# Loading 768 rows at a time instead of 384 in a diagonal prefix-sum kernel that streams 285 MB

## Chip, cores, metric

One core of a Trainium2 chip. Kernels are compared only within the same rounds. The metric is the device time of that core in microseconds. The span of a profile, from its first to its last instruction, is mostly some 1.7 us shorter than the time of the same run.

## The reference

```python
def setup_inputs():
    B, H, W = 4, 4224, 4224
    return {"x": np.random.randn(B, H, W).astype(np.float32)}

def reference(x):
    ps = np.cumsum(np.cumsum(x, axis=1), axis=2)
    diag = np.diagonal(ps, axis1=1, axis2=2)
    return np.cumsum(diag, axis=1).astype(np.float32)
```

Every value below or above the diagonal counts, so all of x, 4 x 4224 x 4224 x 4 = 285.47 MB, has to be read; the result is 68 KB.

## The kernel before

Rows are loaded in groups of 384 (3 to a partition), converted to bf16 on the way, into six rotating buffers. TensorE (PE) sums columns into a small matrix `d` of one row per group; VectorE (DVE) and ScalarE (ACT) share the row sums left of the diagonal; GpSimd (POOL) issues the loads. At the end of a batch the row sums are turned into `d`, and two scans give the output. The last 128 rows of the last batch come in pieces so that little is left to do after the final byte.

```python
P = 128; F = 3; GW = P * F; NG = N // GW; NBUF = 6          # GW = 384, NG = 11
def load_group(b, g):
    t = strips.tile([P, F, N], BF16, name="strip")
    r0 = g * GW
    nc.gpsimd.dma_start(
        out=t, in_=x[b, r0 : r0 + GW, :].rearrange("(p f) w -> p f w", f=F))
    return t
# ... per group g of a batch
for j in range(g + 1, NG):
    for q in range(F):
        columns(j, 0, GW, strip[:, q, j * GW : (j + 1) * GW])    # PE, into d
for q in range(F):
    mu = mup.tile([P, GW], BF16, name="mu")
    masked(mu, strip[:, q, lo:hi], um3[q], ru[:, k, q : q + 1])  # DVE
    columns(g, 0, GW, mu)
    if ws > 0:
        act_sum(sa_at(q), strip[:, q, wp:ws])                    # ACT
row_sums(rs_at, strip[:, :, ws:hi])                              # DVE
if not whole and g == 0:
    diag_b = last.tile([P, P], BF16, name="diag_b")
    nc.gpsimd.dma_start(out=diag_b, in_=x[b, TB:N, TB:N])
# ... at the end of a batch
for q in range(F):
    matmul(d[:, q : GW : F], rows[:, :, q], ident)
# ... last 256 + 128 rows of the last batch
acuts = [(1536, N - HC), (0, 1536)]                              # two pieces of 256 rows
bcuts = [(2432, TB), (1024, 2432), (320, 1024), (0, 320)]        # four pieces of 128 rows
# ... row sums, products with arows, then
row_sums(ttot, tsum[:, : n + 2])
matmul(fin_b, ttot, weights[:, 0:P])                             # then add, store
```

## Time and profile before

| | kernel before |
|---|---|
| time, median of the first 3 runs | 669.16 us (669.05 to 669.71) |
| span of the profile | 667.8 us |
| read from HBM over the span | 428 GB/s |
| transfers on the software queue | 50 (7,456 packets) |
| issue to landing of a 384-row load | 82.6 us |

The busy row of the page shows that no compute engine is near its limit (microseconds, share of the span, instructions):

```profile
PE 229.2 (34%) x862; PEld 96.5 (14%) x862; DVE 253.5 (38%) x371; ACT 153.3 (23%) x249; POOL 33.0 (5%) x72
```

### The profile page before, as it was taken

The page shows a single profiled execution, that of the slowest core. Times are in us where ns is not written, and L with a number is a line of the kernel's source. Part 1 is how long each engine was busy: PE and PEld are TensorE (multiplying, and loading weights), DVE is VectorE, ACT ScalarE, POOL GpSimd, SP SyncE. Part 2 cuts the span into 40 slices and gives each one's busy share as a digit, 9 for nine tenths or more (in the row PEclk, how much of TensorE's full clock was granted, in tenths as well). Part 3 has the DMA queues.
Part 4 walks back from the last instruction along what each step waited for, and adds up shares of the span by engine and source line. Part 5 has one row for each costly group of instructions (what it writes and reads, how often), then busy time and mean ns, then how long its engine had stood idle before and what let it go on. Part 6 is the DMA issues. An engine that isn't in the chain of part 4 may idle for free.

```text
span 667.8 us, 2641 instructions
## 1 busy us (share of the span) xinstructions
PE 229.2 (34%) x862; PEld 96.5 (14%) x862; DVE 253.5 (38%) x371; ACT 153.3 (23%) x249; POOL 33.0 (5%) x72
## 2 busy tenths in 40 slices
PE   0444542211155453221125553322112553322225
PEld 0122211000022221100002221110001221111002
DVE  2123334344623333334472222333457222233357
ACT  0001222233301112223330111222342011122235
POOL 5000000000000000000000000000000000000000
PEclk9977665665577766665557777665555777665668
DMA  9999999999999999999999999999999999999997
GB/s 202 217 219 218 219 219 217 217 216 212 211 221 219 219 219 215 217 219 217 219 217 217 210 216 219 219 219 219 214 216 219 219 217 215 216 216 219 217 207 142
DMA packets 7830, 143.23 MB, mean 214 GB/s; under 512 B 989, under 2 KB 1290, under 8 KB 2314
## 3 DMA queue, kind: packets, MB, share of 16 engines
q0 software_dynamic: 7456, 142.47, 99.7%
q1 hardware_dynamic: 362, 0.61, 0.3%
q8 instruction: 6, 0.10, 0.1%
q14 instruction: 6, 0.05, 0.0%
HBM read 285.47 MB, written 0.07 MB: 428 GB/s over the span
## 4 chain that ended last, share of the span: by engine, by line
another core or an unknown queue 54%; DVE 36%; DMA 7%; PE 1%; issue 1%; POOL 0%; DVEq 0%; POOLq 0%
DVE rs L192 24%; DVE mu L195 9%; DMA strip<-in_x_dram 7%; DVE c L329 1%; PE d L175 1%; DVE parts L192 1%; DVE tsum L192 0%; DVE c L195 0%; POOL strip L70 0%; DVE pu L192 0%; PE carry_ps L175 0%; DVE rows L242 0%; DVE rows L243 0%; DVEq L195 0%
## 5 line engine op out<-in xcount | busy, mean ns | idle before, releaser
L175 PE MATMUL d<-strip,sel 128*11 128x384 bf16 x660 | 183.7, 458 | 367.3 <-DMA strip<-in_x_dram 367.3
L187 ACT ACTIVATE dump<-strip 128x192 bf16<-128x192 bf16 (+13 forms) x124 | 140.5, 1133 | 509.6 <-DMA strip<-in_x_dram 506.9
L195 DVE SCALAR_TENSOR_TENSOR mu<-strip,um 128x384 bf16<-128x384 bf16 x129 | 65.2, 556 | 397.8 <-DMA strip<-in_x_dram 397.8
L175 PEld LDWEIGHTS <-sel 128*11 128x11 bf16 x792 | 90.5, 114 | 530.0 <-issue 508.9
L192 DVE TENSOR_REDUCE rs<-strip 128x3 f32<-128x1152 bf16 (+10 forms) x42 | 163.8, 3899 | 0.0
L175 PE MATMUL d<-mu,sel 128*11 128x384 bf16 x129 | 38.6, 409 | 40.6 <-DVE mu L195 40.6
L70 POOL DMA_DIRECT2D strip<-in_x_dram x43 | 22.9, 536 | 536.0 <-PE d L175 297.1
L187 ACT ACTIVATION_READ_ACCUMULATOR dump<-strip 128x1 f32 x124 | 23.1, 186 | 0.0
L175 PE MATMUL d<-ident,rows 128*11 128x128 f32 x24 | 5.2, 378 | 20.3 <-DVE rows L243 19.9
L195 DVE DVE_READ_ACCUMULATOR mu<-strip,um 128x1 f32 x129 | 10.7, 83 | 0.0
L175 PEld LDWEIGHTS d<-ident,rows 128*11 128x11 f32 x24 | 2.5, 117 | 24.5 <-DVE rows L243 15.0
L175 PE MATMUL fold<-strip,ident_h 128*128 128x480 bf16 (+1 forms) x14 | 4.5, 461 | 1.7 <-DMA strip<-in_x_dram 1.7
L192 DVE TENSOR_REDUCE pu<-d 11x1 f32<-11x384 f32 x4 | 2.2, 545 | 5.1 <-PE d L175 5.1
L329 DVE TENSOR_TENSOR_SCAN c<-ones_row,carry,c 11x384 f32<-11x384 f32 x4 | 4.0, 1006 | 0.1
L329 DVE TENSOR_TENSOR_SCAN c<-ones_row,carry,d 11x384 f32<-11x384 f32 x4 | 4.0, 1001 | 0.1
L308 POOL DMA_DIRECT2D strip<-in_x_dram x4 | 2.1, 536 | 36.0 <-DMA strip<-in_x_dram 22.3
L192 DVE TENSOR_REDUCE parts<-strip 128x3 f32<-128x3072 bf16 x1 | 3.4, 3351 | 0.0
L175 PEld LDWEIGHTS <-ident_h 128*128 128x128 bf16 x20 | 2.1, 114 | 5.2 <-issue 4.8
L192 DVE TENSOR_REDUCE tsum<-strip 128x1 f32<-128x384 bf16 (+2 forms) x4 | 2.0, 490 | 1.2 <-DMA strip<-in_x_dram 1.2
L304 POOL DMA_DIRECT2D strip<-in_x_dram x2 | 1.4, 712 | 15.0 <-PE d L175 15.0
L195 DVE SCALAR_TENSOR_TENSOR c<-d,to_end 11x384 f32<-11x384 f32 x4 | 2.1, 535 | 0.0
L175 PE MATMUL carry_ps<-pu,earlier 11*11 11x2 f32 x8 | 0.7, 159 | 4.1 <-DVE c L195 4.1
(61 smaller groups left out, 27.0 us busy)
## 6 DMA issues: line engine op xcount, KB each, us to landing
strip<-in_x_dram POOLq DMA_DIRECT2D x43, 3168.0 KB, 82.6
strip<-in_x_dram POOLq DMA_DIRECT2D x1, 1080.0 KB, 73.8
strip<-in_x_dram POOLq DMA_DIRECT2D x1, 768.0 KB, 76.8
head<-in_x_dram SPq DMA_DIRECT2D x1, 528.0 KB
strip<-in_x_dram POOLq DMA_DIRECT2D x1, 416.0 KB, 64.4
strip<-in_x_dram POOLq DMA_DIRECT2D x1, 352.0 KB, 65.6
strip<-in_x_dram POOLq DMA_DIRECT2D x1, 176.0 KB, 58.0
strip<-in_x_dram POOLq DMA_DIRECT2D x1, 80.0 KB, 43.5
```

Of the source, the lines that this page charges most:

```text
L70: nc.gpsimd.dma_start(out=t, in_=x[b, r0 : r0 + GW, :].rearrange("(p f) w -> p f w", f=F))
L175: nc.tensor.matmul(o, lhsT=lhsT, rhs=rhs, start=start, stop=False, skip_group_check=True)
L187: nc.scalar.activation(out=dump[:, :w], in_=src, func=ACT.Copy, accum_out=acc)
L192: nc.vector.reduce_sum(out=acc, in_=src, axis=AX.X)
L195: nc.vector.scalar_tensor_tensor(out=o, in0=i, scalar=1.0, in1=m, op0=ALU.mult, op1=ALU.mult, accum_out=acc,)
L304: nc.gpsimd.dma_start(out=part_a[:, :2, c0:c1], in_=src_a[:, :, c0:c1])
L308: nc.gpsimd.dma_start(out=part_b[:, 0, c0:c1], in_=x[b, TB:N, c0:c1])
L329: nc.vector.tensor_tensor_scan(out=c12[:, i, :], data0=ones_row, data1=src, initial=carry[:, i : i + 1], op0=ALU.mult, op1=ALU.add,)
```

## The change

Its intent: fewer and larger transfers. 768 rows come in one load, 6 to a partition, in three buffers of the same total size; the sixth, half-size load of a batch stays at 384 rows. Whole batches keep their groups in natural order, which makes their output one store instead of two. The last 128 rows come in three pieces instead of four. Row sums of 768-row strips lie at another place, so they reach `d` through six more matmuls with a 64-column matrix `halves`.

```diff
-    NBUF = 6
+    NBUF = 3
+    NS = NG // 2
-    mup = ctx.enter_context(tc.tile_pool(name="mup", bufs=4))
+    mup = ctx.enter_context(tc.tile_pool(name="mup", bufs=3))
+    def strip_tile():
+        return strips.tile([P, F2, N], BF16, name="strip")
+    def load_rows(o, b, r0):
+        f = o.shape[1]
+        nc.gpsimd.dma_start(
+            out=o, in_=x[b, r0 : r0 + f * P, :].rearrange("(p f) w -> p f w", f=f))
# ... (cut: 768-wide masks, add_up() for 3 or 6 rows to a partition, two group orders)
+        for q in range(F2):
+            matmul(d[:, q : GW : F2], r6[:, :NG, q], halves)
         for q in range(F):
-            matmul(d[:, q : GW : F], rows[:, :, q], ident)
+            matmul(d[:, q : GW : F], r3[:, :, q], ident)
-            bcuts = [(2432, TB), (1024, 2432), (320, 1024), (0, 320)]
+            bcuts = [(2432, TB), (640, 2432), (0, 640)]
         nc.sync.dma_start(
-            out=out[b, :T0].rearrange("(g i) -> g i", i=GW), in_=c12[1:NG, 1, :]
+            out=out[b, : j1 * GW].rearrange("(g i) -> g i", i=GW),
+            in_=c12[t0:NG, 1, :],
         )
         if whole:
-            nc.sync.dma_start(out=out[b, T0:N].unsqueeze(0), in_=c12[0:1, 1, :])
             continue
-        shares = [(768, 512), (512, 512), (256, 224)]
+        shares = [(768, 512), (768, 512), (0, 320)]
```

More of the change, by code (lines that the diff above doesn't have):

```diff
@@ L36 @@
     F = 3
+    F2 = 2 * F
     GW = P * F
@@ L65 @@
     nc.sync.dma_start(out=head, in_=src_a[:, :, N - HC : N])
-    def load_group(b, g):
-        t = strips.tile([P, F, N], BF16, name="strip")
-        r0 = g * GW
+    def strip_tile():
+        return strips.tile([P, F2, N], BF16, name="strip")
+    def load_rows(o, b, r0):
+        f = o.shape[1]
         nc.gpsimd.dma_start(
-            out=t, in_=x[b, r0 : r0 + GW, :].rearrange("(p f) w -> p f w", f=F)
+            out=o, in_=x[b, r0 : r0 + f * P, :].rearrange("(p f) w -> p f w", f=f)
         )
-        return t
-    prefetched = {(0, g): load_group(0, g) for g in range(NBUF)}
-    def row_of(j):
-        return (j + 1) % NG
+    prefetched = []
+    for i in range(NBUF):
+        t = strip_tile()
+        load_rows(t, 0, i * F2 * P)
+        prefetched.append(t)
     sel = consts.tile([P, 2 * NG - 1], BF16, name="sel")
@@ L83, with upper_mask @@
     nc.vector.memset(sel[:, NG - 1 : NG], 1.0)
-    def selector(j):
-        k = row_of(j)
-        return sel[:, NG - 1 - k : 2 * NG - 1 - k]
-    def upper_mask(name, q, f):
-        um = consts.tile([P, GW], BF16, name=name)
-        nc.vector.memset(um, 1.0)
+    def upper_mask(f):
+        w = f * P
+        wide = consts.tile([P, w + f - 1], BF16, name=f"um{f}")
+        nc.vector.memset(wide, 1.0)
         nc.gpsimd.affine_select(
-            out=um,
-            in_=um,
+            out=wide,
+            in_=wide,
             compare_op=ALU.is_gt,
             fill=0.0,
-            base=-q,
-            pattern=[[1, GW]],
+            base=1 - f,
+            pattern=[[1, w + f - 1]],
             channel_multiplier=-f,
         )
-        return um
-    um3 = [upper_mask(f"um3_{q}", q, F) for q in range(F)]
-    um1 = upper_mask("um1", 0, 1)
+        return [wide[:, f - 1 - q : f - 1 - q + w] for q in range(f)]
+    um6 = upper_mask(F2)
+    um3 = upper_mask(F)
+    um1 = consts.tile([P, GW], BF16, name="um1")
+    nc.vector.memset(um1, 1.0)
+    nc.gpsimd.affine_select(
+        out=um1,
+        in_=um1,
+        compare_op=ALU.is_gt,
+        fill=0.0,
+        base=0,
+        pattern=[[1, GW]],
+        channel_multiplier=-1,
+    )
     ident = consts.tile([P, P], FP32, name="ident")
@@ L116 @@
     )
+    HP = P // 2
+    halves = consts.tile([P, HP], FP32, name="halves")
+    nc.vector.tensor_add(out=halves, in0=ident[:, :HP], in1=ident[:, HP:])
     ones_row = consts.tile([NG, GW], FP32, name="ones_row")
@@ L120, in counted @@
     def counted(name, rows, width, pieces):
-        ti = consts.tile([rows, width], I32, name=name + "_i")
+        ti = consts.tile([P, GW], I32, name="counted")[:rows, :width]
         for c0, c1, base, step, cm in pieces:
@@ L135, with between_groups @@
     to_end = counted("to_end", NG, GW, [(0, GW, GW, -1, 0)])
-    earlier = consts.tile([NG, NG], FP32, name="earlier")
-    nc.gpsimd.memset(earlier, 1.0)
-    apart = counted(
-        "apart",
-        NG,
-        NG,
-        [(0, 1, GW * LG, GW, -GW), (1, NG, 0, GW, -GW)],
-    )
-    for t in (earlier, apart):
-        nc.gpsimd.affine_select(
-            out=t[:, 1:NG],
-            in_=t[:, 1:NG],
-            compare_op=ALU.is_gt,
-            fill=0.0,
-            base=1,
-            pattern=[[1, NG - 1]],
-            channel_multiplier=-1,
-        )
-        nc.gpsimd.memset(t[0:1, :], 0.0)
+    def between_groups(name, turned):
+        t0 = 1 if turned else 0
+        earlier = consts.tile([NG, NG], FP32, name="earlier" + name)
+        nc.gpsimd.memset(earlier, 1.0)
+        pieces = [(t0, NG, -GW * (1 - t0), GW, -GW)]
+        if turned:
+            pieces.append((0, 1, GW * LG, GW, -GW))
+        apart = counted("apart" + name, NG, NG, pieces)
+        for t in (earlier, apart):
+            nc.gpsimd.affine_select(
+                out=t[:, t0:NG],
+                in_=t[:, t0:NG],
+                compare_op=ALU.is_gt,
+                fill=0.0,
+                base=t0,
+                pattern=[[1, NG - t0]],
+                channel_multiplier=-1,
+            )
+            if turned:
+                nc.gpsimd.memset(t[0:1, :], 0.0)
+        return earlier, apart
+    order_whole = between_groups("_w", False)
+    order_last = between_groups("_l", True)
     weights = counted("weights", P, GW, [(0, GW, 1, 1, -1)])
@@ L203, in masked, with scalar_cols @@
         )
-    def scalar_cols(g):
-        return 0 if g == 0 else (g * GW) * 9 // 16 // 32 * 32
+    def scalar_cols(r0):
+        return r0 * 9 // 16 // 32 * 32
+    rows6, rows3 = [], []
+    for i in range(2):
+        rows6.append(consts.tile([P, NG + 1, F2], FP32, name=f"rows6_{i}"))
+        rows3.append(consts.tile([P, NG, F], FP32, name=f"rows3_{i}"))
+        nc.vector.memset(rows6[i], 0.0)
+        nc.vector.memset(rows3[i], 0.0)
     asum = last.tile([P, 2, 5], FP32, name="asum")
-    tsum = last.tile([P, 11], FP32, name="tsum")
+    tsum = last.tile([P, 8], FP32, name="tsum")
     hs = last.tile([P, 3], FP32, name="hs")
@@ L222, with row_of @@
         whole = b < LB
-        ng = NG if whole else LG
+        t0 = 0 if whole else 1
+        r6, r3 = rows6[b % 2], rows3[b % 2]
         d = psum_d.tile([NG, GW], FP32, name="d")
         first = [True]
+        if not whole:
+            nc.vector.memset(r6, 0.0)
+            nc.vector.memset(r3, 0.0)
+        def row_of(j):
+            return (j + t0) % NG
         def columns(j, lo, hi, rhs):
-            matmul(d[:, lo:hi], selector(j), rhs, start=first[0])
+            k = row_of(j)
+            matmul(
+                d[:, lo:hi], sel[:, NG - 1 - k : 2 * NG - 1 - k], rhs, start=first[0]
+            )
@@ L230, in columns @@
             first[0] = False
-        rs = smalls.tile([P, NG, F], FP32, name="rs")
-        ru = smalls.tile([P, NG, F], FP32, name="ru")
-        sa = smalls.tile([P, NG, F], FP32, name="sa")
-        rows = smalls.tile([P, NG, F], FP32, name="rows")
-        nc.vector.memset(sa[:, row_of(0), :], 0.0)
-        if not whole:
-            nc.vector.memset(rows[:, row_of(LG), :], 0.0)
-        def sum_up(k0, k1):
-            ks = slice(k0, k1)
-            nc.vector.tensor_add(out=rows[:, ks], in0=rs[:, ks], in1=sa[:, ks])
-            nc.vector.tensor_sub(out=rows[:, ks], in0=rows[:, ks], in1=ru[:, ks])
@@ L245 @@
-        for g in range(ng):
-            lo, hi = g * GW, (g + 1) * GW
-            k = row_of(g)
-            strip = prefetched.pop((b, g), None)
-            if strip is None:
-                strip = load_group(b, g)
-            for j in range(g + 1, NG):
-                for q in range(F):
-                    columns(j, 0, GW, strip[:, q, j * GW : (j + 1) * GW])
-            final = not whole and g == ng - 1
-            if not final:
-                wp, ws = 0, scalar_cols(g)
-                sa_at = lambda q: sa[:, k, q : q + 1]
-                rs_at = rs[:, k, :]
-            else:
-                wp, ws = 1280, 1280 + 1536
-                sum_up(1, k)
-                parts = last.tile([P, F, 4], FP32, name="parts")
-                sa_at = lambda q: parts[:, q, 0:1]
-                rs_at = parts[:, :, 1]
-                fold_g = psum_s.tile([P, F, 160], FP32, name="fold")
-                fold_in(fold_g, strip, 0, wp, 160, start=True)
-            for q in range(F):
-                mu = mup.tile([P, GW], BF16, name="mu")
-                masked(mu, strip[:, q, lo:hi], um3[q], ru[:, k, q : q + 1])
-                columns(g, 0, GW, mu)
-                if ws > 0:
-                    act_sum(sa_at(q), strip[:, q, wp:ws])
-            row_sums(rs_at, strip[:, :, ws:hi])
-            if not whole and g == 0:
@@ new lines, in add_up @@
+        def add_up(strip, f, r0, acc, ums, wp=0, ws=None):
+            nw = f * P // GW
+            g = r0 // GW
+            hi = r0 + f * P
+            for j in range(g + nw, NG):
+                for q in range(f):
+                    columns(j, 0, GW, strip[:, q, j * GW : (j + 1) * GW])
+            if ws is None:
+                ws = scalar_cols(r0)
+            for q in range(f):
+                mu = mup.tile([P, F2 * P], BF16, name="mu")[:, : f * P]
+                masked(mu, strip[:, q, r0:hi], ums[q], acc[:, q, 2:3])
+                for h in range(nw):
+                    columns(g + h, 0, GW, mu[:, h * GW : (h + 1) * GW])
+                if ws > wp:
+                    act_sum(acc[:, q, 0:1], strip[:, q, wp:ws])
+            row_sums(acc[:, :, 1], strip[:, :, ws:hi])
@@ new lines, with sum_up @@
+        acc6 = smalls.tile([P, NS, F2, 3], FP32, name="acc6")
+        acc3 = smalls.tile([P, 2, F, 3], FP32, name="acc3")
+        nc.vector.memset(acc6[:, 0, :, 0], 0.0)
+        def sum_up(acc):
+            nc.vector.tensor_add(
+                out=acc[..., 1], in0=acc[..., 1], in1=acc[..., 0]
+            )
+            nc.vector.tensor_sub(
+                out=acc[..., 1], in0=acc[..., 1], in1=acc[..., 2]
+            )
+        ns = NS if whole else NS - 1
+        for s in range(ns):
+            strip = prefetched.pop(0) if prefetched else None
+            if strip is None:
+                strip = strip_tile()
+                load_rows(strip, b, s * F2 * P)
+            add_up(strip, F2, s * F2 * P, acc6[:, s], um6)
+            if not whole and s == 0:
@@ L276 @@
                 diag_b = last.tile([P, P], BF16, name="diag_b")
                 nc.gpsimd.dma_start(out=diag_b, in_=x[b, TB:N, TB:N])
-            if not whole and g == 1:
+            if not whole and s == 1:
                 row_sums(hs[:, 2:3], diag_b)
@@ L285 @@
                     columns(LG, h * P, GW, hmu[:, h, : GW - h * P])
+        a6 = acc6[:, :ns]
+        sum_up(a6)
+        for h in range(2):
+            ps = slice(h * HP, (h + 1) * HP)
+            k = row_of(h)
+            nc.vector.tensor_copy(
+                out=r6[ps, k : k + 2 * ns : 2, :], in_=a6[ps, :, :, 1]
+            )
+        strip = strip_tile()
         if whole:
-            sum_up(0, NG)
-        else:
+            load_rows(strip[:, :F], b, T0)
+            add_up(strip[:, :F], F, T0, acc3[:, 0], um3)
+            sum_up(acc3[:, 0])
+            nc.vector.tensor_copy(out=r3[:, LG, :], in_=acc3[:, 0, :, 1])
+        else:
+            for h in range(2):
+                load_rows(strip[:, h * F : h * F + F], b, T0 - (2 - h) * GW)
+            add_up(strip[:, :F], F, T0 - 2 * GW, acc3[:, 0], um3)
+            sum_up(acc3[:, 0])
+            nc.vector.tensor_copy(out=r3[:, row_of(LG - 2), :], in_=acc3[:, 0, :, 1])
+            fold_g = psum_s.tile([P, F, 160], FP32, name="fold")
+            wp, ws = 1280, 1280 + 1536
+            fold_in(fold_g, strip[:, F:], 0, wp, 160, start=True)
+            parts = last.tile([P, F, 4], FP32, name="parts")
+            add_up(strip[:, F:], F, T0 - GW, parts, um3, wp, ws)
@@ L290 @@
             nc.vector.tensor_scalar_mul(
-                out=parts[:, :, 2], in0=ru[:, k, :], scalar1=-1.0
+                out=parts[:, :, 2], in0=parts[:, :, 2], scalar1=-1.0
             )
             row_sums(parts[:, :, 3], fold_g)
-            row_sums(rows[:, k, :], parts)
+            row_sums(r3[:, row_of(LG - 1), :], parts)
+        for q in range(F2):
+            matmul(d[:, q : GW : F2], r6[:, :NG, q], halves)
         for q in range(F):
-            matmul(d[:, q : GW : F], rows[:, :, q], ident)
+            matmul(d[:, q : GW : F], r3[:, :, q], ident)
@@ L299 @@
         if not whole:
-            part_a = strips.tile([P, F, N], BF16, name="strip")
+            strip = strip_tile()
+            part_a = strip[:, 0:2]
+            part_b = strip[:, 2]
             acuts = [(1536, N - HC), (0, 1536)]
             for c0, c1 in acuts:
-                nc.gpsimd.dma_start(out=part_a[:, :2, c0:c1], in_=src_a[:, :, c0:c1])
-            part_b = strips.tile([P, F, N], BF16, name="strip")
-            bcuts = [(2432, TB), (1024, 2432), (320, 1024), (0, 320)]
+                nc.gpsimd.dma_start(out=part_a[:, :, c0:c1], in_=src_a[:, :, c0:c1])
@@ L307 @@
+            bcuts = [(2432, TB), (640, 2432), (0, 640)]
             for c0, c1 in bcuts:
-                nc.gpsimd.dma_start(out=part_b[:, 0, c0:c1], in_=x[b, TB:N, c0:c1])
+                nc.gpsimd.dma_start(out=part_b[:, c0:c1], in_=x[b, TB:N, c0:c1])
             fold_a = psum_s.tile([P, 2, 256], FP32, name="fold_a")
@@ L312 @@
             cp, ca = c0 + 768, c0 + 768 + 1152
-            fold_in(fold_a, part_a[:, :2], c0, cp, 256, start=True)
+            fold_in(fold_a, part_a, c0, cp, 256, start=True)
             for h in range(2):
                 act_sum(asum[:, h, 1:2], part_a[:, h, cp:ca])
-            row_sums(asum[:, :, 2], part_a[:, :2, ca:c1])
+            row_sums(asum[:, :, 2], part_a[:, :, ca:c1])
         pu = smalls.tile([NG, 2], FP32, name="pu")
@@ L322 @@
         masked(c12[:, 1, :], d, to_end, pu[:, 1:2])
+        earlier, apart = order_whole if whole else order_last
         carry_ps = psum_s.tile([NG, 2], FP32, name="carry_ps")
@@ L336 @@
             )
+        j1 = NG - t0
         nc.sync.dma_start(
-            out=out[b, :T0].rearrange("(g i) -> g i", i=GW), in_=c12[1:NG, 1, :]
+            out=out[b, : j1 * GW].rearrange("(g i) -> g i", i=GW),
+            in_=c12[t0:NG, 1, :],
         )
         if whole:
-            nc.sync.dma_start(out=out[b, T0:N].unsqueeze(0), in_=c12[0:1, 1, :])
             continue
@@ L346 @@
         cp = c0 + 768
-        fold_in(fold_a, part_a[:, :2], c0, cp, 256)
+        fold_in(fold_a, part_a, c0, cp, 256)
         for h in range(2):
@@ L357 @@
         fin_b = psum_s.tile([1, P], FP32, name="fin_b")
-        shares = [(768, 512), (512, 512), (256, 224)]
+        shares = [(768, 512), (768, 512), (0, 320)]
         n = 1
         for i, ((c0, c1), (wp, wa)) in enumerate(zip(bcuts, shares)):
-            fold_in(fold_b, part_b[:, 0], c0, c0 + wp, 256, start=i == 0)
-            act_sum(tsum[:, n : n + 1], part_b[:, 0, c0 + wp : c0 + wp + wa])
-            row_sums(tsum[:, n + 1 : n + 2], part_b[:, 0, c0 + wp + wa : c1])
+            fold_in(fold_b, part_b, c0, c0 + wp, 256, start=i == 0)
+            act_sum(tsum[:, n : n + 1], part_b[:, c0 + wp : c0 + wp + wa])
+            if i == 2:
+                row_sums(tsum[:, n + 2 : n + 3], fold_b)
+            row_sums(tsum[:, n + 1 : n + 2], part_b[:, c0 + wp + wa : c1])
             n += 2
@@ L369 @@
                 matmul(fin_a[:, P : 2 * P], arows[:, 1:2], weights[:, 0:P])
-        row_sums(tsum[:, n : n + 1], fold_b)
-        c0, c1 = bcuts[3]
-        row_sums(tsum[:, n + 1 : n + 2], part_b[:, 0, c0:c1])
         ttot = last.tile([P, 1], FP32, name="ttot")
-        row_sums(ttot, tsum[:, : n + 2])
+        row_sums(ttot, tsum)
         matmul(fin_b, ttot, weights[:, 0:P])
```

## The prediction

> **What bounds the kernel now.** I began with the page's 40 slices, because an average over the whole span would hide a stage with another limit.
>
> ```profile
> span 667.8 us, 2641 instructions
> ...
> DVE  2123334344623333334472222333457222233357
> ...
> DMA  9999999999999999999999999999999999999997
> GB/s 202 217 219 218 219 219 217 217 216 212 211 221 219 219 219 215 217 219 217 219 217 217 210 216 219 219 219 219 214 216 219 219 217 215 216 216 219 217 207 142
> ...
> q0 software_dynamic: 7456, 142.47, 99.7%
> ...
> HBM read 285.47 MB, written 0.07 MB: 428 GB/s over the span
> ```
>
> All sixteen DMA engines are busy in every slice but the last; VectorE (DVE), the busiest compute engine, never passes 7 tenths. The 285.47 MB are exactly 4 x 4224 x 4224 x 4 bytes: x is read once, so there are no bytes to save. (The GB/s row counts the bf16 bytes written, half of those read.)
>
> Next come the waits. The engines wait for loads, not the loads for the engines:
>
> ```profile
> ACT dump L187 <- DMA strip<-in_x_dram: 506.9, 42, 33.5
> DVE mu L195 <- DMA strip<-in_x_dram: 397.8, 43, 12.3
> PE d L175 <- DMA strip<-in_x_dram: 367.3, 40, 20.7
> POOL strip L70 <- PE d L175: 297.1, 21, 16.7
> POOL strip L70 <- DVE rs L192: 193.6, 13, 15.0
> ```
>
> The last two rows look like a buffer limit and are not one. The list of issues gives 82.6 us from the issue of a 384-row load to its landing, while one load takes 15 us: about five others are ahead of it. A buffer freed a few us later would just stand less long in the queue.
>
> Then the rate of the loads, from the times at which ScalarE (ACT), which waits for each strip, starts:
>
> ```profile
> 35.59 0.36 ACT L187 ACTIVATE dump<-strip 128x192 bf16<-128x192 bf16 x1 [33.49 <-DMA strip<-in_x_dram]
> 484.60 1.80 ACT L187 ACTIVATE dump<-strip 128x1920 bf16<-128x1920 bf16 x1 [9.67 <-DMA strip<-in_x_dram]
> 499.56 1.99 ACT L187 ACTIVATE dump<-strip 128x2144 bf16<-128x2144 bf16 x1 [9.21 <-DMA strip<-in_x_dram]
> 530.24 0.36 ACT L187 ACTIVATE dump<-strip 128x192 bf16<-128x192 bf16 x1 [24.38 <-DMA strip<-in_x_dram]
> ```
>
> The first two are loads 1 and 31: (484.60 - 35.59) / 30 = 14.967 us for 384 x 16,896 = 6.488 MB, or 433.5 GB/s. This holds straight through two batch ends, so the batch ends cost nothing today. From 499.56 to 530.24 there are two loads and 30.68 us, 0.75 more than 2 x 14.967: that is the 128-row diagonal block in 512-byte pieces, which the change keeps.
>
> **What the Trainium skill says.** "DMA: Bandwidth & Descriptors", section "Where 436 GB/s comes from", puts the ceiling at 435.2 GB/s. The trace agrees: 433.5 is 99.6% of it. Section "Measured" of that page has 341 GB/s for 1 MB and 425 for 16 MB and advises batches of at least 1 MiB; the loads here read 6.2 MiB already and stand behind one another, so the small-transfer loss is not in this trace, and 12.4 MiB has little left to win. Section "Anatomy of one DMA" gives some 2 us fixed cost, mostly completion; in this trace that shows once at the end of the queue, not per load: the whole gap between 14.967 and 6.488 MB / 435.2 = 14.908 is 0.059 us. Section "Latency and other measured facts" warns of row pitches at large powers of two. The pitch between partitions goes from 50,688 to 101,376 bytes, 99 x 1,024, far from a power of two; I expect no loss.
>
> **The change, part by part.** *Bytes:* the same.
>
> *Descriptors.* The built program gives a 768-row load as 128 partitions x 2 x 12,672 values, so each piece remains 50,688 bytes: the change does not make longer pieces. Packets before can be rebuilt: 43 x 128 + 128 + 2 x 256 + 4 x 128 = 6,656 pieces, plus one completion on each of 16 engines for each of 50 transfers, 800: 7,456, just what the queue shows. After: three batches of 5 x 256 + 128, then 4 x 256 + 2 x 128 + 128 + 2 x 256 + 3 x 128, together 6,528 pieces; 30 transfers add 480: 7,008. What really goes is twenty transfers.
>
> *Worth of a transfer.* If the 0.059 us is a cost per transfer, 20 x 0.059 = 1.2 us is gained. The last pieces land at about 649.83, 655.0, 658.66, 660.67, 662.35 and 663.23; against 2.212, 1.573, 0.852, 0.721 and 0.360 MB at 435.2 the gaps hold 0.10, 0.04, 0.05, 0.02 and 0.05 us too much: about constant, though the sizes differ sixfold, which speaks for a cost per transfer. But the jitter is as large, and a cost per piece or a slightly lower rate would gain nothing. I take 0.5 us (estimate, below half way).
>
> *Queue depth.* Six buffers of 15 us become three of 30: still 152 KB a partition. With three, a freed buffer finds two loads ahead, less the compute time. Heaviest compute per 768 rows, estimated: first strip, PE 54 column matmuls at 0.262 (30 took 7.86 us at 185.24) is 14.1; VectorE must wait there with its last three masks, because three mask buffers replace four, then 3 x 0.9 us and a reduction of 6 x 768 values at 0.96 per ns, 4.8: 22 us in all. Fifth strip: six masks 5.4 us and a reduction of 12,672 values 13.2: 19 us. Both are under the 29.9 us that a strip takes to land. The shortest queue is at the fifth strip of a batch: 15 us (the half-size sixth load) + 30 - 19 = 26 us left when its buffer is freed. Never dry: cost 0.
>
> *Masks, extra matmuls.* Each 768-wide mask gives two matmuls instead of one, some 60 more PE instructions of about 0.3 us, 18 us over the span, and the copies of row sums some 0.2 us each: all under the loads. Stores: 3 fewer, beside the loads: 0. Start: three prefetches instead of six, the first with 256 pieces (a 256-piece issue took 712 ns at the end, a 128-piece one 536): at most 0.2 us later, while the head load of 0.54 MB fills the engines. First compute comes at about 35.6 us instead of 20.6, which costs nothing.
>
> *The end.* The last 384-row half lands as before, but then the row sums cross into d by six matmuls with the halves matrix (12 PE passes) before the three old ones.
>
> ```profile
> 655.41 0.17 DVE L192 TENSOR_REDUCE rows<-parts 128x3 f32<-128x12 f32 x1
> 655.63 0.83 PE L175 MATMUL d<-ident,rows 128*11 128x128 f32 x6 [0.32 <-DVE rows L192]
> 656.50 0.55 DVE L192 TENSOR_REDUCE pu<-d 11x1 f32<-11x384 f32 x1 [0.36 <-PE d L175]
> 662.36 0.55 DVE L192 TENSOR_REDUCE tsum<-strip 128x1 f32<-128x384 bf16 x1 [0.90 <-DMA strip<-in_x_dram]
> 663.23 0.39 DVE L192 TENSOR_REDUCE tsum<-strip 128x1 f32<-128x224 bf16 x1 [0.31 <-DMA strip<-in_x_dram]
> 663.90 0.48 DVE L192 TENSOR_REDUCE tsum<-strip 128x1 f32<-128x320 bf16 x1
> 664.48 0.16 DVE L192 TENSOR_REDUCE ttot<-tsum 128x1 f32<-128x9 f32 x1
> ```
>
> Six passes took 0.83, 0.14 each; twelve narrower ones at 0.09 to 0.14 are 1.1 to 1.7 us, of which 0.32 fills the wait shown: d is 0.8 to 1.4 later, say 1.0. So is VectorE up to the scans, but it stood idle 0.90 + 0.31 us for part_b pieces, which eats most of it. I follow it on: second scan done at 661.15 instead of 660.15, sum of fold_a and arows to 661.95, first piece to 662.45; the new second piece (1,792 columns, 0.92 MB) lands near 662.8, its 512 columns take to 663.5; PE, held by the four products with arows until 663.25, ends its fold at 663.7; fold sum to 664.15; last 320 columns to 664.55; ttot at 664.6, against 664.48. One piece fewer and one reduction fewer thus just pay for the halves matmuls: +0.1 us. From ttot to the span's end 3.3 us as before.
>
> Sum: -0.5 + 0.1 = -0.4 us: **668.7 us**.
>
> **Rivals.** *The full per-transfer saving:* 1.2 us, about 668.0; for it the even gaps at the end, against it their jitter. *End bound by VectorE:* if the twelve passes take 0.14 each and nothing is saved per transfer, ttot comes 0.5 us later: 669.6. *Queue runs dry with three coarse buffers:* would need a strip's compute above some 45 us, against 22 by the group durations; if the lower clock doubled PE's time at batch starts it would still hold. A wrong sum here would cost 5 us or more at each batch, 680 or above. *Larger access stride slows HBM or an engine:* 1% would be 6.5 us, 675; nothing in the trace speaks for it, nor can it exclude it. *Large gain:* impossible; 285.47 MB at 435.2 is 656 us, plus some 3 us of start and 4 of end, 663.
>
> **Range and chances.** The kernel before repeats within 0.7 us (669.05 to 669.71). Saving 0 to 1.2, end -0.1 to +0.5, noise 0.4: 667.5 to 670.1. Two per cent is 13.4 us, out of reach for a gain; for a loss only the dry queue or the stride would do it.
>
> **What would show it.** Right: software queue with 7,008 packets; whole strips landing 29.85 to 29.93 us apart; issue to landing of a 768-row load well above 40 us everywhere; no slice before the last two below 200 GB/s; d complete about 1 us later after the last half's landing, ttot within 0.3 us. Wrong: a slice with a dip at the batch ends (queue dry), strips landing over 30.0 us apart (stride), or ttot more than 0.5 us later after that landing (end).

## The result

| | before | changed |
|---|---|---|
| time, median of 6 runs | 669.52 us (669.05 to 670.45) | 668.91 us (668.63 to 669.72) |
| ratio | | 0.9992, 95% interval 0.9979 to 1.0005 |
| the same again, later (`e9_after_again`) | 669.38 us, 9 runs | 669.58 us, 5 runs; 1.0002, 0.9988 to 1.0015 |

A ratio is the mean time of one kernel's runs over that of the other's runs of the same rounds, so it is not quite the ratio of the medians. The first measurement has the changed kernel 0.6 us ahead, the second 0.2 us behind: by the clock the two kernels are the same.

The page of the changed kernel, the same rows as for the kernel before:

```profile
span 667.0 us, 2828 instructions
...
DVE  2043617366924351745883415266398241635687
...
DMA  9999999999999999999999999999999999999997
GB/s 203 219 219 219 218 219 219 217 217 216 208 215 219 219 219 217 216 219 219 219 219 215 216 211 217 220 219 216 216 216 219 220 215 218 216 215 219 216 207 144
...
q0 software_dynamic: 7008, 142.47, 99.7%
...
HBM read 285.47 MB, written 0.07 MB: 428 GB/s over the span
```

The DMA row is unchanged to the digit, the packets are the 7,008 that were worked out, and the rate is still 428 GB/s. VectorE now works in longer bursts (slices of 8 and 9), still under the loads. Its waits have grown, because 768-wide masks wait for PE to free a mask buffer (engine, line, releaser: total us, times, longest):

```profile
DVE mu L218 <- DMA strip<-in_x_dram: 222.3, 20, 25.8
DVE mu L218 <- PE d L198: 91.9, 16, 9.0
```

Those 91.9 us cost nothing: they lie inside the 30 us that the next strip needs. The list of issues (KB each, us from issue to landing) shows how far ahead of need the loads still are:

```profile
strip<-in_x_dram POOLq DMA_DIRECT2D x19, 6336.0 KB, 69.6
strip<-in_x_dram POOLq DMA_DIRECT2D x5, 3168.0 KB, 55.3
```

ACT's waits give the landings again; strips 3 and 4 of the first batch:

```profile
125.29 1.27 ACT L210 ACTIVATE dump<-strip 128x1280 bf16<-128x1280 bf16 x1 [23.62 <-DMA strip<-in_x_dram]
155.18 1.64 ACT L210 ACTIVATE dump<-strip 128x1728 bf16<-128x1728 bf16 x1 [21.56 <-DMA strip<-in_x_dram]
```

29.89 us for 768 rows, inside the 29.85 to 29.93 forecast; the kernel before takes 29.93. Of the eleven such intervals that ACT's waits show in this trace nine are 29.87 to 29.91. The other two, 30.89 and 30.14, are over the 30.0 that the prediction named as a sign of a harmful stride, but are no such sign: in each a fetch of instructions is recorded (at 69.61 and 459.22), and there the spread between the earliest and the latest DMA engine jumps from 0.43 to 1.39 us and from 1.38 to 1.62. One engine was held up, and the landing waits for the slowest. The shortest time from issue to landing of a 768-row load is some 54 us.

**What a transfer costs, exactly.** The trace also holds a record of every piece, the contiguous run of bytes (50,688 here) that one DMA engine moves at a time. The records name no engine; sorted by start they are taken sixteen at a time, one piece for each engine. The first start of such a sixteen, for every eighth, in us:

```
piece          56        64        72        80        88     steps
before    108.871   123.828   138.784   153.741   168.697    14.957 14.956 14.957 14.956
changed   108.579   123.537   138.472   153.430   168.386    14.958 14.935 14.958 14.956
```

In the kernel before every step of eight pieces crosses the end of a transfer. In the changed kernel the step from 64 to 72 lies inside a 768-row load: it is 21 ns shorter, just eight times the 1.867 us from piece to piece. So a transfer end costs each engine 21 to 22 ns, and the completion packets themselves are recorded with 22 ns. Twenty transfers fewer are 20 x 0.0215 = 0.43 us, against the 0.5 us estimated. That is what the change gains in the loads. (Averaged over the sixteen engines, the pieces near the end of the stream start 0.54 us sooner than in the kernel before, in this trace and in that of `e9_after_again`.)

**The end.** These lines answer to those of the prediction (`ttot` is the last sum before the closing product); the last half landed at 649.67 here, at 649.87 before (ACT's wait in both):

```profile
654.79 1.22 PE L198 MATMUL d<-halves,rows 128*11 128x64 f32 x12
655.21 0.17 DVE L215 TENSOR_REDUCE rows<-parts 128x3 f32<-128x12 f32 x1
655.85 0.82 PE L198 MATMUL d<-ident,rows 128*11 128x128 f32 x6
656.71 0.55 DVE L215 TENSOR_REDUCE pu<-d 11x1 f32<-11x384 f32 x1 [0.78 <-PE d L198]
662.62 0.69 DVE L215 TENSOR_REDUCE tsum<-strip 128x1 f32<-128x512 bf16 x1 [0.94 <-DMA strip<-in_x_dram]
663.22 0.41 DVE L215 TENSOR_REDUCE tsum<-fold 128x1 f32<-128x256 f32 x1
...
664.13 0.16 DVE L215 TENSOR_REDUCE ttot<-tsum 128x1 f32<-128x8 f32 x1
```

The twelve passes with `halves` started before the last row sums were ready (654.79 against 655.21) and took 0.10 us each. From landing to the reduction of `d` it is 7.04 us against 6.63, so 0.41 later and not 1.0, and VectorE then waits 0.94 us for the second piece anyway. From landing to `ttot` it is 14.46 us against 14.61.

There is a gain after the last store that the prediction had not reckoned with. From its landing to the end of the span the kernel before takes 1.28 us (666.48 to 667.76), the changed one 0.91 (666.13 to 667.04). SyncE checks the semaphores of the transfers one after another there, 0.06 us apart: in the kernel before six checks come after that of the last store, in the changed kernel none, since its last store has the semaphore that is checked last. It is the same in every trace: 1.27 and 1.28 us in the two with the old stores, 0.90 to 0.92 in the ten with the new ones. So of the 0.72 us between the two spans 0.20 are the earlier landing, 0.15 the sums up to `ttot` and 0.37 this.

### The profile page after: what moved, and what is told of

Same layout as the page of the kernel before. It is cut to its first block, busy times and chain, and to the rows that moved or that the text cites. A ratio compares the mean times of both kernels' runs of the same rounds, so it can differ in the third digit from the quotient of the medians.

```text
span 667.0 us, 2828 instructions
## 1 busy us (share of the span) xinstructions
PE 215.1 (32%) x967; PEld 97.2 (15%) x967; DVE 336.3 (50%) x376; ACT 140.1 (21%) x225; POOL 27.0 (4%) x56
## 3 DMA queue, kind: packets, MB, share of 16 engines
q0 software_dynamic: 7008, 142.47, 99.7%
HBM read 285.47 MB, written 0.07 MB: 428 GB/s over the span
## 4 chain that ended last, share of the span: by engine, by line
another core or an unknown queue 42%; DVE 25%; PE 23%; DMA 5%; issue 4%; DVEq 0%; POOLq 0%
PE d L198 23%; DVE acc L215 17%; DVE mu L218 7%; DMA strip<-in_x_dram 5%; PE fold L198 1%; DVE pu L215 0%; DVE c L397 0%; DVE c L218 0%; DVE tsum L215 0%; DVE acc L301 0%; DVE acc L304 0%; PE carry_ps L198 0%; DVE rows L331 0%; DVEq L218 0%
## 5 line engine op out<-in xcount | busy, mean ns | idle before, releaser
L218 DVE SCALAR_TENSOR_TENSOR mu<-strip,um 128x768 bf16<-128x768 bf16 (+1 forms) x129 | 110.7, 908 | 314.4 <-DMA strip<-in_x_dram 222.3
L198 PE MATMUL d<-strip,sel 128*11 128x384 bf16 x603 | 140.0, 406 | 344.4 <-DMA strip<-in_x_dram 344.4
L210 ACT ACTIVATE dump<-strip 128x416 bf16<-128x416 bf16 (+8 forms) x112 | 128.4, 1146 | 523.2 <-DMA strip<-in_x_dram 520.2
L215 DVE TENSOR_REDUCE acc<-strip 128x6 f32<-128x4608 bf16 (+6 forms) x23 | 195.9, 8518 | 0.0
L198 PEld LDWEIGHTS <-sel 128*11 128x11 bf16 x849 | 86.1, 101 | 526.3 <-issue 488.4
L198 PE MATMUL d<-mu,sel 128*11 128x384 bf16 x243 | 59.7, 355 | 67.5 <-DVE mu L218 67.4
L75 POOL DMA_DIRECT2D strip<-in_x_dram x24 | 16.5, 687 | 555.5 <-DVE acc L215 414.5
L210 ACT ACTIVATION_READ_ACCUMULATOR dump<-strip 128x1 f32 x112 | 20.9, 186 | 0.0
L198 PE MATMUL d<-halves,rows 128*11 128x64 f32 x48 | 5.7, 304 | 0.0
L198 PEld LDWEIGHTS d<-halves,rows 128*11 128x11 f32 x48 | 5.1, 136 | 2.1 <-issue 2.1
L372 POOL DMA_DIRECT2D strip<-in_x_dram x2 | 1.4, 716 | 29.2 <-DVE acc L215 29.2
```

The source lines that it names most:

```text
L75: nc.gpsimd.dma_start(out=o, in_=x[b, r0 : r0 + f * P, :].rearrange("(p f) w -> p f w", f=f))
L198: nc.tensor.matmul(o, lhsT=lhsT, rhs=rhs, start=start, stop=False, skip_group_check=True)
L210: nc.scalar.activation(out=dump[:, :w], in_=src, func=ACT.Copy, accum_out=acc)
L215: nc.vector.reduce_sum(out=acc, in_=src, axis=AX.X)
L218: nc.vector.scalar_tensor_tensor(out=o, in0=i, scalar=1.0, in1=m, op0=ALU.mult, op1=ALU.mult, accum_out=acc,)
L372: nc.gpsimd.dma_start(out=part_a[:, :, c0:c1], in_=src_a[:, :, c0:c1])
```

## The experiments

Ten runs, all correct. Ratios are to the kernel before.

| run | time, us | before, us | ratio |
|---|---|---|---|
| e1_two_transfers | 669.43 | 669.79 | 0.9991 |
| e2_short_pieces | 673.17 | 669.79 | 1.0049 |
| e8_row_transfers | 674.75 | 669.79 | 1.0072 |
| e4_before_three_buffers | 669.46 | 669.79 | 0.9993 |
| e3_two_buffers | 694.14 | 669.81 | 1.0361 |
| e5_halves_early | 669.86 | 669.81 | 1.0000 |
| e6_four_pieces | 669.77 | 669.81 | 1.0002 |
| e7_right_early | 670.21 | 669.81 | 1.0011 |
| e9_after_again | 669.58 | 669.38 | 1.0002 |
| e10_many_memsets | 669.22 | 669.38 | 1.0004 |

### Transfers, pieces: e1, e2, e8

`e1_two_transfers` undoes the larger load alone:

```diff
-        nc.gpsimd.dma_start(out=o, in_=x[...].rearrange("(p f) w -> p f w", f=f))
+        src = x[b, r0 : r0 + f * P, :].rearrange("(p f) w -> p f w", f=f)
+        for q in range(0, f, F):
+            nc.gpsimd.dma_start(out=o[:, q : q + F], in_=src[:, q : q + F])
```

> The changed kernel with each 768-row load issued as two transfers of the same 50,688-byte pieces: 19 transfers more (49), pieces as before. Theory, a small fixed cost per transfer on each DMA engine: the engine records of both traces show 1,867 ns from piece to piece inside a load and 1,888 across the end of a load, so 21 ns a transfer, 19 x 0.021 = +0.4 us against the changed kernel, about 669.3. First rival, the whole 0.059 us by which a load exceeded the fabric rate belongs to the transfer: +1.1 us, 670.0. Second rival, transfers are free and the gain of the change came from elsewhere: +0.0. In the records 38 of 49 transfers should show the 21 ns step after 8 pieces instead of after 16.

Its ratio of 0.9991 can't be told from the changed kernel's 0.9992. In the records every step of eight pieces is back at 14.957 us (32 pieces from 123.527 to 183.353: 59.826 us; changed kernel 59.784, two transfer ends less). The 21 ns are there; 0.4 us is too little for the clock.

`e2_short_pieces` pads the rows in the buffers, so a piece can't run over a row's end; `e8_row_transfers` has the same pieces but a transfer to each:

```diff
-        return strips.tile([P, F2, N], BF16, name="strip")
+        return strips.tile([P, F2, N + 16], BF16, name="strip")[:, :, :N]
# e8 also, after the first three loads:
+        for q in range(f):
+            nc.gpsimd.dma_start(out=o[:, q : q + 1], in_=src[:, q : q + 1])
```

> The changed kernel with strips padded by 32 bytes a row, so that every piece is one row of 16,896 bytes; transfers stay 30, big pieces per engine go from 344 to 1,032. Theory (a piece costs only the 3 to 4 ns by which 1,867 ns exceeds 50,688 bytes at a sixteenth of 435.2 GB/s): 688 x 0.0035 = +2.4 us, about 671.3. Rival, a piece has a fixed cost of the 22 ns by which the recorded 1,886 ns exceed that: +15 us, 684. Rival, the 3.5 ns are a lower rate and not a cost per piece: +0.

> As e2_short_pieces, but all loads after the first three are issued row by row: the same 16,896-byte pieces, 90 transfers more (120). Against e2_short_pieces: at 21 ns a transfer +1.9 us (about 673.2), at 59 ns +5.3 us, at 0 nothing. A queue that ran dry, since no more than eight transfers can be outstanding, would show as slices well under 200 GB/s and as more than 10 us; I expect none, because eight transfers are 40 us of work.

```profile
GB/s 181 216 217 217 216 215 216 217 217 217 216 216 217 216 217 217 216 216 217 217 215 217 215 217 217 216 215 216 215 217 217 216 216 216 217 217 216 215 214 141
...
q0 software_dynamic: 18016, 142.47, 101.6%
```

The lower of these rows of the page of `e2_short_pieces` has 11,008 packets more: 16 engines x 688. The time is 3.4 us over the kernel before, so some 3.8 over the changed one, more than the 2.4 expected. The records say why. Where nothing disturbs them, these pieces follow each other at 624.7 ns inside a transfer, those of the changed kernel at 1,867.0. Two sizes give two unknowns: 33,792 bytes more take 1,242.3 ns, that is 435.2 GB/s on 16 engines, and 3.5 ns are left as a cost per piece, as expected: 688 x 3.5 ns = 2.4 us. Averaged over the engines, the stream does fall behind the changed kernel by 2.3 us between 13 us and its end. The rest is lost at the start: within the first 10 us the engines are 1.5 us behind (181 GB/s in the first slice, 203 in the changed kernel); in `e8_row_transfers`, with the same first three loads, 0.7 us. What slows the start stays open. Both rivals fall, that of 22 ns a piece (15 us) and that of no cost per piece.

`e8_row_transfers` has 90 transfers more at 1.6 us more: 18 ns each by the clock, 21 by the records (645.9 ns from piece to piece across an end, 624.6 inside a transfer). The rival of 59 ns a transfer (5.3 us) falls. Its queue did not run dry: from the second slice to the last but one none is under 213 GB/s, though in its trace never more than eight transfers are under way and most issues wait for the landing of an earlier one. So 768-row loads could only win by having fewer ends, since their pieces, 50,688 bytes, are those of 384-row loads.

### Queue depth: e4, e3

```diff
# e4: kernel before                    # e3: changed kernel
-    NBUF = 6                          -    NBUF = 3
+    NBUF = 3                          +    NBUF = 2
```

> The kernel before with three buffers of 384 rows instead of six: half the memory, a freed buffer finds two loads ahead (30 us) less some 10 us of compute, 20 us left. Theory, queue depth is in surplus: unchanged, 669.5 within 0.5 us, issue to landing falls from 82.6 to some 35 us. Rival, depth of five loads matters to the rate: slower by more than 2 us.

```profile
strip<-in_x_dram POOLq DMA_DIRECT2D x43, 3168.0 KB, 38.1
```

A load now lands 38.1 us after its issue instead of 82.6, and the time is the same (0.9993). Half of the 152 KB a partition was surplus in the kernel before.

> The changed kernel with two buffers instead of three. In its trace a 768-row buffer is freed 19 to 20 us after its load landed. Theory of the queue: inside a batch the other buffer still has 30 us of load, so 10 us are left and nothing is lost; at the fifth strip of each whole batch the next load is only the half-size sixth (15 us), so the queue is dry for 19.3 - 15 = 4.3 us plus some 2 us until data flows again, three times: +18 to +20 us, about 688, with three dips in the DMA row at the ends of the first three batches and none in the last. Rival, two buffers are as good: 669. Rival, each strip loses because descriptors are issued too late: +2 us at each of some 20 strips, 705 or above.

Page, then the landings (ACT) and issues (POOL) around the first batch end, of `e3_two_buffers`:

```profile
DMA  9999999996999999999699999999969999999996
GB/s 214 215 211 211 234 210 214 220 222 143 185 215 215 221 216 215 214 225 215 142 188 213 228 214 212 219 222 213 214 140 187 215 226 217 211 219 221 214 207 132
```

```profile
170.04 1.99 ACT L210 ACTIVATE dump<-strip 128x2144 bf16<-128x2144 bf16 x1 [4.38 <-DMA strip<-in_x_dram]
174.42 0.70 POOL L75 DMA_DIRECT2D strip<-in_x_dram  x1 [29.35 <-DVE acc L304]
238.03 0.55 ACT L210 ACTIVATE dump<-strip 128x416 bf16<-128x416 bf16 x1 [61.68 <-DMA strip<-in_x_dram]
```

This is what a dry queue looks like: three dips, one at each end of a whole batch, none in the last batch, as the queue model had it. The sizes were short: the half-size load landed at 170.04, the next load could only be issued at 174.42, and two strips later it is 67.99 us instead of the 59.86 of the changed kernel (170.14 to 230.00 there): 8.1 us for this batch end, not 6.3. The 4.4 us from landing to issue were right. The other 3.7 us, where 2 were expected, are in the records, averaged over the engines: they had ended 1.4 us before the landing, their first pieces started 1.5 us after the issue, and these pieces took 0.9 us longer than later ones. The three batch ends, 8.1 to 8.5 us each by the same reckoning, are the 24 to 25 us measured. The third buffer is therefore needed. That a fourth would do nothing follows from the queue model, since with three the DMA row has no dip; it was not run.

### The end of the kernel: e5, e6, e7

`e5_halves_early` moves the six matmuls ahead of the last load's own; `e6_four_pieces` restores the four pieces and their shares; `e7_right_early` loads columns 2432 to 4224 of the last 128 rows where the diagonal block was loaded, and drops the first piece of the end:

```diff
# e5: also in whole batches, after load_rows(strip[:, :F], b, T0)
+            for q in range(F2):
+                matmul(d[:, q : GW : F2], r6[:, :NG, q], halves)
             fold_g = psum_s.tile([P, F, 160], FP32, name="fold")
# e6
-            bcuts = [(2432, TB), (640, 2432), (0, 640)]
+            bcuts = [(2432, TB), (1024, 2432), (320, 1024), (0, 320)]
# e7
-                nc.gpsimd.dma_start(out=diag_b, in_=x[b, TB:N, TB:N])
+                nc.gpsimd.dma_start(out=right_b, in_=x[b, TB:N, CB:N])
-            bcuts = [(2432, TB), (640, 2432), (0, 640)]
+            bcuts = [(640, CB), (0, 640)]
```

> The changed kernel with the six matmuls on the halves matrix issued before the last load's own matmuls, when their operand has long been ready. Theory: d is complete about 0.4 us sooner after the last half landed (7.04 us from landing to its reduction becomes 6.6), but the reduction of the second piece then only waits longer for its transfer (0.94 us becomes some 1.3), so the time stays, 668.9 within 0.4. Rival, the halves matmuls are on the path: -0.4 us with the final sum that much sooner after the landing.

In its trace, whose last half landed at 650.18:

```profile
656.80 0.55 DVE L215 TENSOR_REDUCE pu<-d 11x1 f32<-11x384 f32 x1 [0.36 <-PE d L198]
663.13 0.69 DVE L215 TENSOR_REDUCE tsum<-strip 128x1 f32<-128x512 bf16 x1 [1.35 <-DMA strip<-in_x_dram]
664.64 0.16 DVE L215 TENSOR_REDUCE ttot<-tsum 128x1 f32<-128x8 f32 x1
```

6.62 us to the reduction of `d`, 1.35 us of wait for the piece, and `ttot` 14.46 us after the landing, the same as without the move. The halves matmuls are hidden behind the piece that is still to land.

> The changed kernel with the last 128 rows again in four pieces and the four old shares. Theory, from the trace of the changed kernel: with VectorE free from 661.7, the second piece lands at 662.2, then 0.55, 0.39, 0.43 and 0.48 us of reductions bound by the two small landings: final sum 14.6 us after the last half's landing instead of 14.46, +0.15 us, plus 0.02 for a transfer: time +0.2, hardly to be told from zero by the clock, but visible in the trace. Rival, three pieces were a loss because the last one is larger: -0.2.

The time is that of the others (1.0002). In its trace `ttot` is 15.44 us after the landing, 0.8 later than expected; but the reason is not the pieces: VectorE waits 0.77 us for PE's fold of the last products, and PE worked at half the clock there, see below. Three pieces or four is not decided by this.

> The changed kernel, but the diagonal block of the last 128 rows is not loaded alone in 512-byte pieces: columns 2432 to 4224 of these rows come in one load at that place (7,168-byte pieces) and the first tail piece goes. The 512-byte load held the queue 0.75 us where its bytes need 0.15. Theory: -0.6 us and one transfer less, and the tail has one piece less to sum after the last landing: about 668.2. Rival, the 0.75 us was not the small pieces: 0. A version to beat both kernels, if only by a thousandth.

The rival holds: nothing was gained, 1.0011 (0.9997 to 1.0024). The last half landed at 651.77, 2.10 us later than in the changed kernel, and 1.96 of that are simply the 0.85 MB moved ahead of it; so nothing of a 0.6 us saving is seen. (The total alone would not show it: PE's clock in 664 to 667 us was 0.64 in this trace, and the last addition waited 1.14 us for PE.) The records of the kernel before show what I had misread: on every engine the diagonal block, eight pieces and one end, adds 0.22 us. The rest of the 0.75 us was the slowest engine alone: the spread between the earliest and the latest engine went from 1.29 to 1.75 us around that block, where a fetch of instructions held one of them.

### What remains between equal kernels: e9, e10

> The changed kernel once more, unaltered, to narrow the interval and to see how much its own span moves between chips. Theory: 20 transfers at 21 ns make -0.43 us, so a ratio of 0.9994 to the kernel before, inside the spread of the runs (668.6 to 669.7 the first time). Rival, the change really gains 1 us or more: 0.998 with an interval that excludes 1.

The same program, traced a second time, has a span of 668.4 us instead of 667.0. Of these 1.4 us 0.35 are a later landing of the last half (650.02 instead of 649.67); the other 1.0 is in the last 4 us. Stretches from 661 to 664 us, first of the changed kernel's trace and then of this one (us; busy time and instructions of PE, weight loads, DVE, ACT, POOL; granted clock, DMA share, GB/s):

```profile
661.00:664.00 3.00, 1.74 (x11) 0.90 (x11) 2.00 (x5) 1.46 (x6) 0.00 (x0) 1.00 0.27 49
```

```profile
661.00:664.00 3.00, 3.00 (x13) 1.15 (x12) 1.30 (x3) 1.46 (x5) 0.00 (x0) 0.50 0.28 52
```

and the end of the latter:

```profile
663.79 0.73 PE L198 MATMUL fold<-strip,ident_h 128*128 128x256 bf16 x3
664.55 0.42 DVE L215 TENSOR_REDUCE tsum<-fold 128x1 f32<-128x256 f32 x1 [0.90 <-PE fold L198]
...
665.48 0.16 DVE L215 TENSOR_REDUCE ttot<-tsum 128x1 f32<-128x8 f32 x1
```

At a granted clock of 1.00 the products with `arows` are out of PE's way when the second piece lands; at 0.50 they hold back its fold, VectorE waits 0.90 us, and `ttot` comes 15.46 us after the landing instead of 14.46. So the end of one and the same program is worth 1 us more or less. The trace of `e6_four_pieces` has 0.51 in this stretch, those of the kernel before, e1, e4 and e5 have 1.00, e7 and e10 0.79 and 0.82. The Trainium skill, "TensorE: Matmul & The Clock Gate", Part 1, says that the activity window that opens the clock is free-running, so that the same kernel meets it at different phases; two traces of one program with 1.00 and 0.50 agree with that.

> The changed kernel with 950 one-element memsets added on GpSimd, fifty ahead of each 768-row strip, some 5 us each time, with buffers freed long before they are needed, so that no load is late enough to matter. They lengthen the program. In the records of all traces each 8 KB fetch of instructions holds up one DMA engine by some 0.5 us and each 16 KB fetch by 1.1 us, and a strip lands with its slowest engine. Theory: 950 instructions are some seven more 8 KB fetches, and if they keep to one engine it falls behind by up to 3.5 us: +1.0 to +3.5 us, with the spread of the engines at the last strip up from 2.1 us by that much. Rival, instruction fetches are absorbed: within 0.5 us of the changed kernel of the same call.

```diff
         for s in range(ns):
+            for _ in range(50):
+                nc.gpsimd.memset(scratch, 0.0)
```

```profile
q14 instruction: 14, 0.11, 0.0%
```

The seven fetches were added (the changed kernel has 7 on this queue), but my theory falls: the median is 669.22 us, no slower than the changed kernel of the same call. Only one of five runs, the profiled one, took 671.47 us. In that trace the latest engine started its last strip piece 3.8 us after the earliest, against 2.1 in the changed kernel's trace, so the lag that I expected occurs, but not as a rule. Whether the fetches made it in that run stays open. None of the ten beats the changed kernel beyond the noise, and it does not clearly beat the kernel before.

## Why the prediction was right

*The bound.* Right. The same 285.47 MB at the same rate, in every run with three buffers or more. The 435.2 GB/s cited in the prediction is what the records give when costs per piece and per transfer are taken off.

*Pieces and packets.* Right, 7,008. That a 768-row load has the same pieces as a 384-row one was the fact that decided the case.

*Worth of a transfer.* 0.43 us instead of 0.5; the choice below half of 1.2 us was right for the reason given there: not all that a load takes over its bytes belongs to the transfer. At 435.2 GB/s the bytes are 14.908 us; 8 x 3.5 ns for the pieces and 21 ns for the end make the 14.957 recorded. The other 10 ns of the prediction's 59 lie outside the undisturbed steps; fetches and stores hold engines up there. The even gaps between the last landings, which I read as speaking for a cost per transfer, were too coarse to show it.

*Queue depth.* Right. The shortest time from issue to landing, 54 us, is near the 26 + 30 reckoned. Strips were freed 19 to 20 us after landing, by the issue times, against 22 and 19 estimated; `e3_two_buffers` shows where the margin ends.

*The 0.75 us of the diagonal block.* Wrong, though it did not enter the sum: 0.22 us on an engine, and for the rest one engine held up at that moment. A landing is the slowest of sixteen engines, so one interval between two landings doesn't price one transfer.

*The end.* Right in mechanism (hidden behind the second piece), mis-sized in one term: `d` came 0.41 us later instead of 1.0, as the passes took 0.10 us each and began before the last row sums were ready. `ttot` came 0.15 us sooner after the landing instead of 0.1 later. But the same end takes 1 us longer when PE's clock is at half, which I had not reckoned with. "From ttot to the span's end 3.3 us as before" was wrong: it is 2.9, by the order in which the stores' semaphores are checked.

*The sum.* The forecast was -0.4 us; the first measurement has -0.6, the second +0.2. That the first comes so close is luck: a term of -0.37 was missing, the gain in the loads reached the last landing only in part (-0.20 in one trace of the changed kernel, +0.15 in the other), and both measurements lie within what the clock of the last 4 us and a lagging DMA engine do to one and the same program. That the change gains 0.43 us in the loads is shown by the records; that it makes the kernel faster is not shown. What the prediction had right is the mechanism: nothing large can change here, since bytes, pieces and rate stay.

## What to carry to other kernels

When a stream of loads already runs at 99.6% of the fabric and its loads stand in a queue, larger loads can only save the ends between them; price one end (here 21 ns) and multiply before writing anything. Check first whether the larger load really has longer pieces. Size buffers by the load that is still ahead when a buffer is freed, at the worst place (here the half-size load at the end of a batch), and remember that running dry costs more than the lateness of the issue (here 8.1 us for 4.4).

## What the Trainium skill lacked or had wrong

- "DMA: Bandwidth & Descriptors", "Anatomy of one DMA": it calls the bubble of the completion write about one cycle on trn2. Here a transfer end costs every engine 21 to 22 ns, in all traces looked at. Its fixed 2 us per transfer doesn't apply to a transfer that stands behind others, which adds only these 21 ns; when the queue had run dry (`e3_two_buffers`), 1.5 us passed from issue to the first pieces and 0.36 us from the last completion record to the waiting engine's start.
- The same page, "Why small descriptors are slow (HBM only)", has a fixed overhead of some 3 cycles per packet, told for small descriptors, and no time for large pieces: here 3.5 ns for each piece of 16,896 or 50,688 bytes, the rest at 435.2 GB/s.
- "Runtime: NRT & Kernel Launch", "Instruction fetch mechanics", calls the cost of crossing a 16 KiB block one that is mostly hidden. It has no figure for the DMA side: there a 16 KB fetch is recorded with 0.89 to 0.98 us and an 8 KB one with 0.32, in front of a load's next piece. Ordinarily the total doesn't show it (`e10_many_memsets`).
- That a transfer has landed only when all its engines are done is in the pages; how far the engines drift apart over a kernel is in none: by 1.7 to 3.8 us at the last strip here.
